# First feed-forward product by seven block products: weight-block sums on VectorE, residual rows on GpSimd

## The chip, the cores and the metric

One core of a Trainium2 chip runs the whole kernel. The metric is device time in microseconds (us) of one execution; the profile beside it is one execution taken by the hardware profiler.

## The reference

One decoder layer over 512 tokens of width 2048, all in float32. The change touches the second half, from the first normalisation to the hidden layer of the feed-forward part:

```python
        x = layer_norm(DEEPNORM_ALPHA * x + mix, ln_mix_g[layer], ln_mix_b[layer])
        f = jnp.square(jax.nn.relu(x @ w_ff1[layer])) @ w_ff2[layer]
        x = layer_norm(DEEPNORM_ALPHA * x + f, ln_ff_g[layer], ln_ff_b[layer])
```

Here x is 512 x 2048, `w_ff1` 2048 x 8192 and `w_ff2` 8192 x 2048. Ahead of it stand the input product, two token mixers (attention and pooling), the gates and the output product.

## The kernel before

**Split products.** Every float32 operand of a large product is split into a high part (an fp32r copy made on ScalarE, line 86) and a low part (operand minus high part, on VectorE, line 87). A product is three matmuls: high x high, high x low, low x high. Weights stream through `wr` (loaded on SP's queue), `wh` and `wl`, three buffers of each. A step of a product takes two 128-row slices of weight by 512 columns, 24 matmuls. `fill` issues the split of step i + 2 ahead of the matmuls of step i, so the third buffer comes free when the matmuls of step i - 1 end. `late` is a list of closures; one is popped in each step. The order on each engine is the order in which the code is written.

**First feed-forward product (line 146).** 16 groups of 512 hidden channels. A group is 16 slices of the contraction x 4 blocks of 128 channels x 3 = 192 matmuls, weights stationary, the 512 tokens moving. Group 0 is done in two halves of 256 tokens (`F[0]`, `F[1]`), while the first normalisation (`ln1_norm`, transposes `ln1_t`) of the other half runs beside it. When a group ends, `ff1_evac` takes four PSUM tiles through Relu and Square on ScalarE into `hpR`, and puts two closures on `late`. Each (`parts`) makes four sums of 256 columns on VectorE (line 498), a high part `hpH` of 7 x 256 columns on ScalarE, a low part `hpL` on VectorE, and two stores to `h_parts` on GpSimd's DMA queue. The last two groups need no sums (`plain_parts`).

**Second product (line 615).** It reads `h_parts` back and already works by 2 x 2 x 2 blocks with seven products for seven chunks of 1024 hidden channels; the last chunk (line 660) is plain. Its weight sums are VectorE operations on 128 x 2048 (lines 585 to 596).

**Residual.** `ln1_finish` multiplies and adds the normalisation's weights to `acc` in natural layout on VectorE (line 479), and `y_save` stores the rows to `y_parts` with some columns subtracted; they seed the accumulators of the second product.

Everything is one program order per engine; nothing is reordered.

Of the kernel before, what the change touches and what calls it, by code (L numbers as in the profile page):

```python
# [35 lines left out]
C_MADD, C_CNT, C_ID, C_RC, C_IF, C_W = 0, 512, 1024, 1152, 1216, 1217  # L36

# [30 lines left out]
def decoder_layer(ctx: ExitStack, tc: tile.TileContext, x, xt, positions, w_in, w_pool, pool_scale,  # L68
                  w_branch_attn, w_branch_pool, w_out, ln_mix_g, ln_mix_b, w_ff1, w_ff2,
                  ln_ff_g, ln_ff_b, consts, vectors, out, h_parts, h_rest, y_parts):  # L70
# [6 lines left out]
    cst = G.tile([P, C_W], F32, name="cst")  # L77
# [5 lines left out]
    ident = cst[:, C_ID:C_ID + P]  # L83
# [9 lines left out]
    # ---------------------------------------------------------------- streamed products  # L93
# [101 lines left out]
    # ---------------------------------------------------------------- x, given transposed  # L195
    L1s = ExitStack()
    L1 = L1s.enter_context(tc.tile_pool(name="L1", bufs=1))
    xs = []
# [15 lines left out]
    # ---------------------------------------------------------------- queue of all products  # L214
# [6 lines left out]
    # pooling branch  # L221
# [33 lines left out]
    def pool_diff(g):  # L255
        s, u = pooled[g], uu.pop(g)
        d = s
        rc = cst[:, C_RC + 16 * g:C_RC + 16 * g + 16]
# [32 lines left out]
    # attention  # L291
    rope = {}

    def rope_tables():
# [4 lines left out]
        nc.vector.tensor_scalar(ang, ang, cst[:, C_IF:C_IF + 1], None, op0=OP.mult)  # L299
# [45 lines left out]
    def s1a(i):  # L345
# [7 lines left out]
        nc.vector.tensor_add(sm[i][:, :n], p[:, :n], cst[:, o:o + n])  # L353
# [4 lines left out]
    def s1b(i):  # L358
# [3 lines left out]
        nc.vector.scalar_tensor_tensor(sm[i][:, :n], sm[i][:, :n], 1.0, cst[:, o:o + n], op0=OP.mult,  # L362
# [71 lines left out]
    # output projection, residual and normalisation  # L434
# [19 lines left out]
    def ln1_norm(t0):  # L454
        for t in (t0, t0 + 1):
            ln_stat(t)
        for t in (t0, t0 + 1):
            nc.vector.tensor_scalar(acc[t], acc[t], mv[:, t, 0:1], mv[:, t, 3:4],
                                    op0=OP.subtract, op1=OP.mult)

    def ln1_t(t0, j):
        p = PS.tile([P, 2, 2 * P], F32, name="sc" if j % 2 else "tp", bufs=1)
        y = L2["p"].tile([P, 2, 2 * P], F32, name="rl", bufs=2)
        for e in range(2):
            k = 2 * j + e
            for t in range(2):
                nc.tensor.transpose(p[:, e, t * P:(t + 1) * P], acc[t0 + t][:, k * P:(k + 1) * P], ident)  # L467
        for e in range(2):
# [9 lines left out]
    def ln1_finish(t, op, v):  # L478
        nc.vector.tensor_tensor(acc[t], acc[t], L2[v], op=op)

    def y_save(t):
        if t < 2:
            for n in (1, 3):
                c = slice(n * 512, (n + 1) * 512)
                nc.vector.tensor_tensor(acc[t + 2][:, c], acc[t + 2][:, c], acc[t][:, c], op=OP.subtract)
        nc.gpsimd.dma_start(y_parts[t], acc[t])
# [4 lines left out]
    # the hidden layer: its blocks (tokens x channels) 11 12 21 22 and the sums that the second product takes  # L491
    # slots: 21, 11, 22, 12, then S1 = 21 + 22, S2 = S1 - 11, S3 = 11 - 21, S4 = 12 - S2; the last chunk needs no sums
    def ff1_evac(g):
        def parts(j):
            a, b, c = ("h1", "h2", "h3") if j else ("h4", "h5", "h6")
            r = R[j]
            for d, x0, x1, op in ((4, 0, 2, OP.add), (5, 4, 1, OP.subtract), (6, 1, 0, OP.subtract), (7, 3, 5, OP.subtract)):
                nc.vector.tensor_tensor(r[:, d], r[:, x0], r[:, x1], op=op)
            h = L2["p"].tile([P, 7, 256], F32R, name="hpH", tag=b)
            l = L2["p"].tile([P, 7, 256], F32R, name="hpL", tag=c)  # L500
            split(h, l, r[:, 1:])
            for e, v in enumerate((h, l)):
                nc.gpsimd.dma_start(h_parts[g // 2, e, :, :, 2 * (g % 2) + j].rearrange("s p f -> p s f"), v.bitcast(F32))

        def plain_parts():
            h = L2["p"].tile([P, 2, 4, 256], F32R, name="hpH", tag="h5")
            l = L2["p"].tile([P, 2, 4, 256], F32R, name="hpL", tag="h6")
            split(h, l, R["all"])
            for e, v in enumerate((h, l)):
                for j in range(2):  # L510
                    nc.gpsimd.dma_start(h_rest[e, :, :, 2 * (g % 2) + j], v[:, j].bitcast(F32))

        R = {}

        def f(b, p):
            if not R:
                if g < 14:
                    for j in range(2):
                        R[j] = L2["p"].tile([P, 8, 256], F32, name="hpR", tag=("h4", "h1")[j])
                else:  # L520
                    R["all"] = L2["p"].tile([P, 2, 4, 256], F32, name="hpR", tag="h4")
                    R[0], R[1] = R["all"][:, 0], R["all"][:, 1]
            t = lambda b: R[b % 2][:, 2 * (b // 2):2 * (b // 2) + 2]
            nc.scalar.activation(t(b), p, AF.Relu)  # L524
            if b == 3:
                for b in range(4):
                    nc.scalar.activation(t(b), t(b), AF.Square)
                late.extend([lambda: parts(0), lambda: parts(1)] if g < 14 else [plain_parts])
# [3 lines left out]
    # second product, by blocks of 2 x 2 x 2 with seven products  # L532
    MO = (("11", 1), ("21", 3), ("22", 7), ("11", 4), ("E", 6), ("22", 5), ("21", 2))
    first_tags = {"11": "w0", "21": "w1", "22": "w2", "12": "w3", "E": "w4"}
# [3 lines left out]
    def h_load(c, m):  # L538
        v = L2["p"].tile([P, 2, 4, 256], F32R, name="hop", tag=f"h{m}")
# [4 lines left out]
    def w_rows(c, k):  # L544
        """Rows of the second weight that block row k of chunk c takes: two tiles from each group of 512."""
        return w_ff2[c * 1024:(c + 1) * 1024].rearrange("(a k b p) n -> k p a b n", a=2, k=2, b=2)[k]

    class Unit:
# [11 lines left out]
        def give(self, role, new):  # L560
            """The tile of a role that is done goes to a role of the next unit."""
# [67 lines left out]
    def bcast(v):  # L629
        return bass.AP(tensor=v.tensor, offset=v.offset, ap=[[0, P], [1, DM]])  # L630

    def tail_load(m):
        if m < 4:
            rest[m] = L2["p"].tile([P, 2, 4, 256], F32R, name="hop", tag=f"h{m}")
            for e in range(2):
                nc.gpsimd.dma_start(rest[m][:, e], h_rest[e, :, m])
        elif m < 6:
            rest[m] = L2["p"].tile([P, DM], F32, name="ln", tag=f"h{m}")
# [38 lines left out]
    def block(t, n):  # L677
        """Row t, columns n * 512 on of the sum that the last normalisation takes."""
# [18 lines left out]
    # ---------------------------------------------------------------- the order of the products  # L697
# [20 lines left out]
    F += [add(cols(w_ff1, n * 512), 16, "ws", yact, ff1_evac(n)) for n in range(1, 16)]  # L718
# [5 lines left out]
    units[0].tag = dict(first_tags)  # L724
# [5 lines left out]
    steps += pieces + ends  # L730

    # ---------------------------------------------------------------- emission
# [172 lines left out]
```

## Time and profile before

| | |
|---|---|
| median of 3 runs | 2449.92 us (2448.81 to 2450.59) |
| span of the profiled execution, first to last instruction | 2448.5 us |
| PE busy | 2433.2 us, 99% |
| VectorE (DVE) busy | 1303.0 us, 53% |
| ScalarE (ACT) busy | 851.9 us, 35% |
| GpSimd (POOL) busy | 130.7 us, 5% |
| matmuls | 10936 |
| moved by DMA | 383.29 MB, mean 157 GB/s |

For the profiled execution the span is the time that is given; it lies 1.4 us (0.06%) under the median. PE is TensorE's matmuls, PEld its weight loads, SP and POOL also issue DMAs. PE counts as busy from a matmul's start to its modelled end, and matmuls overlap, so what one costs is read from the distance of two starts.

### The profile page before, as it was taken

How to read it: one execution, taken by the hardware profiler on the slowest of the kernel's cores; microseconds unless marked ns; L12 is line 12 of the kernel's file. 1: busy time of each engine (PE TensorE's matmuls, PEld its weight loads, DVE VectorE, ACT ScalarE, POOL GpSimd, SP SyncE). 2: the span in 40 equal slices, each digit the busy share in tenths (PEclk: the TensorE clock that was granted, in tenths of full speed). 3: DMA queues.
4: the chain of work that ended last, by engine and by line, in shares of the span. 5: the costliest groups of instructions: out<-in, count | busy, mean ns of one | idle time of the engine just before them, and what ended most of it. 6: DMA issues, size and time to landing. Idle time of an engine off the chain costs nothing.

```text
span 2448.5 us, 26732 instructions
## 1 busy us (share of the span) xinstructions
PE 2433.2 (99%) x10936; PEld 2010.9 (82%) x10936; DVE 1303.0 (53%) x1409; ACT 851.9 (35%) x952; POOL 130.7 (5%) x188
## 2 busy tenths in 40 slices
PE   9999999999999999999999999999999999999998
PEld 7888888877788888889888888888888888888886
DVE  4532245555522335356653334343347988889887
ACT  4323321244422222137434333343334333333330
POOL 0000000000000000000110101000021000110000
PEclk9999999999999999999999999999999999999999
DMA  6333333322233333465665645546677457575652
GB/s 217 87 94 99 103 96 95 95 78 78 71 93 97 101 95 116 125 198 167 195 243 166 217 155 196 183 160 210 241 262 261 160 186 240 206 240 168 210 164 94
DMA packets 166842, 383.29 MB, mean 157 GB/s; under 512 B 11200, under 2 KB 12224, under 8 KB 165696
## 3 DMA queue, kind: packets, MB, share of 16 engines
q1 hardware_dynamic: 133408, 257.84, 33.5%
q0 software_dynamic: 30720, 117.45, 13.8%
q10 hardware_dynamic: 2592, 6.29, 0.8%
q8 instruction: 86, 1.41, 0.2%
q14 instruction: 36, 0.29, 0.0%
HBM read 317.58 MB, written 63.96 MB: 156 GB/s over the span
## 4 chain that ended last, share of the span: by engine, by line
PE 97%; DVE 1%; DMA 1%; ACT 0%; issue 0%; SPq 0%; POOLq 0%; DVEq 0%
PE mm L146 71%; PE pp L615 20%; PE pp L660 4%; PE sc L349 1%; PE tp L381 1%; DMA w<-in_w_ff 1%; DVE wl L87 0%; PE tp L373 0%; PE tp L275 0%; PE sc L275 0%; DVE part L621 0%; DMA wr<-in_w_in 0%; PE sc L467 0%; PE tp L467 0%; ACT wh L86 0%
## 5 line engine op out<-in xcount | busy, mean ns | idle before, releaser
L87 DVE TENSOR_TENSOR wl<-wr,wh 128x1024 fp32r<-128x1024 f32 (+1 forms) x348 | 423.3, 1221 | 891.5 <-ACT wh L86 890.9
L146 PE MATMUL mm<-aH,wh 128*128 128x512 f32 (+1 forms) x1984 | 768.8, 387 | 0.8 <-ACT wh L86 0.6
L146 PE MATMUL mm<-aH,wl 128*128 128x512 f32 (+1 forms) x1984 | 759.4, 383 | 0.2 <-DVE wl L87 0.2
L146 PE MATMUL mm<-aL,wh 128*128 128x512 f32 (+1 forms) x1984 | 758.7, 382 | 0.0
L86 ACT ACTIVATE wh<-wr 128x1024 fp32r<-128x1024 f32 (+1 forms) x348 | 367.0, 1055 | 878.2 <-PE mm L146 809.0
L615 PE MATMUL pp<-wh,hop 128*128 128x512 f32 x1568 | 483.1, 389 | 0.7 <-ACT hpR L524 0.7
L146 PEld LDWEIGHTS mm<-aH,wh 128*128 128x128 f32 x1984 | 373.2, 188 | 76.4 <-ACT wh L86 2.3
L146 PEld LDWEIGHTS mm<-aL,wh 128*128 128x128 f32 x1984 | 373.2, 188 | 74.3 <-issue 1.9
L146 PEld LDWEIGHTS mm<-aH,wl 128*128 128x128 f32 x1984 | 373.0, 188 | 73.9 <-DVE wl L87 1.1
L615 PEld LDWEIGHTS pp<-wh,hop 128*128 128x128 f32 x1568 | 294.4, 188 | 62.0 <-ACT hpR L524 1.1
L86 ACT ACTIVATE wh<-w 128x1024 fp32r<-128x1024 f32 x196 | 208.1, 1062 | 313.6 <-PE pp L615 295.5
L615 PE MATMUL pp<-wl,hop 128*128 128x512 f32 x784 | 305.2, 389 | 1.0 <-DVE wl L87 1.0
L87 DVE TENSOR_TENSOR wl<-w,wh 128x1024 fp32r<-128x1024 f32 x196 | 238.4, 1222 | 71.4 <-ACT wh L86 64.3
L615 PEld LDWEIGHTS pp<-wl,hop 128*128 128x128 f32 x784 | 147.2, 188 | 32.4 <-DVE wl L87 1.9
L146 PE MATMUL mm<-wh,aH 128*128 128x512 f32 x384 | 149.9, 390 | 0.0
L146 PE MATMUL mm<-wl,aH 128*128 128x512 f32 x384 | 149.5, 389 | 0.0
L146 PE MATMUL mm<-wh,aL 128*128 128x512 f32 x384 | 149.5, 389 | 0.0
L621 DVE TENSOR_TENSOR part<-part,pp 128x1024 f32<-128x1024 f32 x92 | 112.1, 1218 | 12.7 <-PE pp L615 12.7
L87 DVE TENSOR_TENSOR hpL<-hpR,hpH 128x1792 fp32r<-128x1792 f32 (+1 forms) x30 | 61.3, 2044 | 52.1 <-ACT hpH L86 52.1
L146 PEld LDWEIGHTS mm<-wl,aH 128*128 128x128 f32 x384 | 72.1, 188 | 15.2 <-DVE wl L87 0.4
L146 PEld LDWEIGHTS mm<-wh,aL 128*128 128x128 f32 x384 | 72.1, 188 | 15.1
L146 PEld LDWEIGHTS mm<-wh,aH 128*128 128x128 f32 x384 | 72.1, 188 | 14.7
(143 smaller groups left out, 1700.1 us busy)
## 6 DMA issues: line engine op xcount, KB each, us to landing
wr<-in_w_ff SPq DMA_DIRECT2D x152, 512.0 KB, 3.9
wr<-in_w_in SPq DMA_DIRECT2D x127, 512.0 KB, 3.7
w<-in_w_ff SPq DMA_DIRECT2D x112, 512.0 KB, 6.1
hop<-h_parts POOLq DMA_DIRECT2D x98, 512.0 KB, 7.2
h_parts<-hpH POOLq DMA_DIRECT2D x28, 896.0 KB, 5.7
h_parts<-hpL POOLq DMA_DIRECT2D x28, 896.0 KB, 7.7
wr<-in_w_out SPq DMA_DIRECT2D x40, 512.0 KB, 3.7
wr<-in_w_branch_pool SPq DMA_DIRECT2D x16, 512.0 KB, 3.6
```

Source lines behind the costliest of these rows:

```text
L86: nc.scalar.activation(dst_h, src, AF.Copy)
L87: nc.vector.tensor_tensor(dst_l, src, dst_h.bitcast(F32), op=OP.subtract)
L146: nc.tensor.matmul(o, l, r, start=first and j == 0, stop=last and j == 2)
L349: nc.tensor.matmul(p[:, :n], qT[h][:, qb * P:(qb + 1) * P], kT[h][:, :n], start=True, stop=True)
L381: nc.tensor.matmul(p[:, k * P:], vt["v"][:, k, h * HD:(h + 1) * HD], pT[h][:, k, k * P:], start=k == 0, stop=k == 3)
L615: nc.tensor.matmul(u.ps[:, t], l, r, start=q + j == 0, stop=q == 3 and j == 2)
L621: nc.vector.tensor_tensor(p, p, u.ps, op=OP.add)
L660: nc.tensor.matmul(o, l, r, start=first and i == 0, stop=last and i == 2)
```

## The change

Groups 1 to 15 of the first feed-forward product are computed by 2 x 2 x 2 blocks: the tokens in halves of 256, the contraction in halves of 1024, the group's channels in halves of 256. Seven products M1 to M7 take the place of eight. Each is 2 pieces of 24 matmuls with 256 moving columns.

- The activation sums P1 to P4 are made once, in `F[1]` (`y_sums`, `y_p3`), on VectorE and ScalarE.
- The weight sums are made in each group, four additions of 128 x 2048 on VectorE in place (`sum`). Weight blocks are loaded as 1024 x 256 tiles (`get`, `give`); the tile of a block that is done goes to the next group.
- Products accumulate in three PSUM banks: M1, M6, M7 and M4 in one, M5 and M3 in the second, M2 in the third. In between, a bank's sum so far is copied out (`evac`: M1, M5 and M6 by a ScalarE copy, M7 by a VectorE operation).
- Group 1 takes the products in the order `ORDER1`, groups 2 to 15 in `ORDER`.
- The split of the hidden layer's parts (`h_parts_out`) keeps its operations; `hpH` now has one buffer (tag t10) for all, and the low part is written over `hpR`.
- `ln1_finish` and `y_save` go. The normalised rows are stored to `y_norm`, and `y_rows` loads 128 x 512 chunks of them back and finishes them on GpSimd, 16 chunks in groups 1 to 9.
- The attention masks get a tile of their own, and tags of the tiles are renamed.

```diff
+        k, c0 = int(role[0]) - 1, self.g * 512 + (int(role[1]) - 1) * 256
+        nc.sync.dma_start(self.b[role], w_ff1[k * 1024:(k + 1) * 1024, c0:c0 + 256].rearrange("(a p) n -> p a n", p=P))
...
-    def ln1_finish(t, op, v):
-        nc.vector.tensor_tensor(acc[t], acc[t], L2[v], op=op)
...
+    def y_sums():
+
+        return [lambda: (y_add("22", "22", "21", OP.subtract), y_sum("P1", "22")),
+                lambda: (y_add("21", "11", "21", OP.subtract), y_add("11", "11", "22", OP.add)),
+                lambda: (y_add("12", "11", "12", OP.subtract), y_sum("P2", "11")),
+                lambda: y_sum("P4", "12")]
...
+    def y_rows(t, n):
+        c = slice(n * 512, (n + 1) * 512)
+        v, g, b = low["u"][:, 1], low["g"][:, 0], low["g"][:, 1]
+        tt = nc.gpsimd.tensor_tensor
+        nc.gpsimd.dma_start(v, y_norm[t, :, c])
...
+        tt(v, v, g, op=OP.mult)
+        tt(v, v, b, op=OP.add)
+        nc.gpsimd.tensor_scalar(v, v, ALPHA, None, op0=OP.mult)
+        if t >= 2 and n % 2:
+            nc.gpsimd.dma_start(g, y_parts[t - 2, :, c])
+            tt(v, v, g, op=OP.subtract)
+        nc.gpsimd.dma_start(y_parts[t, :, c], v)
...
+    def h_parts_out(g, j):
+        r = R[g][:, j]
+        for d, x0, x1, op in ((4, 0, 2, OP.add), (5, 4, 1, OP.subtract), (6, 1, 0, OP.subtract), (7, 3, 5, OP.subtract)):
+            nc.vector.tensor_tensor(r[:, d], r[:, x0], r[:, x1], op=op)
+        h = L2["p"].tile([P, 7, 256], F32R, name="hpH", tag="t10")
+        split(h, r[:, 1:], r[:, 1:])
+        for e, v in enumerate((h.bitcast(F32), r[:, 1:])):
+            nc.gpsimd.dma_start(h_parts[g // 2, e, :, :, 2 * (g % 2) + j].rearrange("s p f -> p s f"), v)
...
+    ORDER = ("M1", "M2", "M5", "M3", "M6", "M7", "M4")
+    ORDER1 = ("M1", "M5", "M6", "M3", "M7", "M2", "M4")
+    FACTORS = {"M1": ("11", "11"), "M5": ("P1", "11"), "M6": ("P2", "11"), "M3": ("P4", "22"), "M7": ("P3", "12"),
+               "M2": ("12", "21"), "M4": ("22", "11")}
...
+            split(self.h, self.l, b[FACTORS[self.what][1]][:, 4 * (j % 2):4 * (j % 2) + 4])
+            if j % 2:
+                for o, i in {"M1": (("11", "12"),), "M5": (("11", "22"),), "M6": (("11", "21"),)}.get(self.what, ()):
+                    u.sum(o, i)
+            elif self.what == "M3":
+                u.sum("12", "22")
...
+            p = u.ps[{"M3": "M5", "M2": "M2", "M5": "M5"}.get(what, "M1")]
+            for n in range(2):
+                o = p[:, n * 256:(n + 1) * 256]
+                for k in range(4):
...
+            def block(slot, in0, in1, op):
+                r = R[u.g][:, :, slot]
+                tt(r, in0.rearrange("p (n t) -> p n t", n=2), in1, op=op)
+                act(r, r, AF.Relu)
+
+            if what == "M1":
+                act(m1, ps["M1"], AF.Copy)
+            elif what == "M5":
+                act(m5, ps["M5"], AF.Copy, scale=-1.0)
+            elif what == "M6":
+                act(u2, ps["M1"], AF.Copy, scale=-1.0)
+            elif what == "M3":
+                h_rows(u.g)
+            elif what == "M7":
+                block(3, m5, v["M1"], OP.subtract)
+            elif what == "M4":
+                act(R[u.g][:, :, 1], v["M1"], AF.Relu)
+                act(R[u.g][:, :, :4], R[u.g][:, :, :4], AF.Square)
+                late.extend(h_out(u.g))
...
+    for p in fpieces:
+        fill(pos[2])
+        if late:
+            late.pop(0)()
+        if p.u is funits[0] and p.j == 0:
+            y_p3()
+            funits[0].get("21")
+        p.mult()
+        pos[2] += 1
+        if p.j == 2 and chunks:
+            y_rows(*chunks.pop(0))
+        elif p.j == 8 and chunks and p.u.g < 8:
+            y_rows(*chunks.pop(0))
```

Three places in the engines' orders. First VectorE's order around the end of a group in the middle of the first product, before: `wl` is the low part of the weights, `hpR` takes the four sums, `hpL` is the low part of the hidden layer's parts.

```order
L87 TENSOR_TENSOR wl<-wr,wh 128x1024 x7
L498 TENSOR_TENSOR hpR<-hpR 128x256 x4
L87 TENSOR_TENSOR hpL<-hpR,hpH 128x1792
L87 TENSOR_TENSOR wl<-wr,wh 128x1024
L498 TENSOR_TENSOR hpR<-hpR 128x256 x4
L87 TENSOR_TENSOR hpL<-hpR,hpH 128x1792
L87 TENSOR_TENSOR wl<-wr,wh 128x1024 x7
```

The same place now, from the end of group 6 on; `w_10296` and the like are the weight blocks, `low` holds the copies of banks, L608 is the sum of two weight blocks.

```order
L90 TENSOR_TENSOR wl<-w_10296,wh 128x1024 x2
L608 TENSOR_TENSOR w_10296<-w_10296,w_10424 128x2048
L90 TENSOR_TENSOR wl<-w_10356,wh 128x1024
L543 TENSOR_TENSOR hpR<-hpR 128x256 x4
L90 TENSOR_TENSOR hpR<-hpR,hpH 128x1792
L90 TENSOR_TENSOR wl<-w_10356,wh 128x1024
L543 TENSOR_TENSOR hpR<-hpR 128x256 x4
L90 TENSOR_TENSOR hpR<-hpR,hpH 128x1792
L90 TENSOR_TENSOR wl<-w_10296,wh 128x1024 x2
L608 TENSOR_TENSOR w_10296<-w_10296,w_10485 128x2048
L90 TENSOR_TENSOR wl<-w_10485,wh 128x1024
L608 TENSOR_TENSOR w_10424<-w_10424,w_10485 128x2048
```

The pieces' low parts, the two bundles of parts and their order are as before; the weight sums stand between them, and each `wl` now feeds 24 matmuls of 256 columns in place of 24 of 512.

Second, TensorE's order in group 6 now: the last matmul of M5 and the first of M3, then the same of M6 and M7, of M7 and M4, with what a row waits for; the numbers name buffers, `mm_10267` and `mm_10134` are banks, `ysH` and `aH` high parts of activations.

```order
L646 MATMUL mm_10267<-ysH_7700,wl_10234 128x256
L646 MATMUL mm_10267<-ysH_7799,wh_10262 128x256 [waits Activation_49]
...
L646 MATMUL mm_10134<-ysH_7767,wl_10352 128x256
L646 MATMUL mm_10134<-aH_5948,wh_10385 128x256 [waits Activation_49]
...
L646 MATMUL mm_10134<-aH_5988,wl_10421 128x256
L646 MATMUL mm_10134<-aH_6028,wh_10453 128x256 [waits DVE_49,Activation_49]
```

Each pair adds to the same bank, and between the two the bank is read: by ScalarE's copies of `mm_10267` and of `mm_10134` in the first two pairs, by VectorE's operation on `mm_10134` in the third. Before, a bank was read only when its group had ended, and the next group took other banks.

Third, GpSimd's queue behind the stores of a group's parts, now; before, only stores and loads stood there.

```order
L547 DMA h_parts<-hpR 128x7x256
L522 DMA low<-y_norm 128x512
L523 DMA low<-in_ln_mix_g 128x512
L524 DMA low<-in_ln_mix_b 128x512
L525 TENSOR_TENSOR low<-low 128x512
L526 TENSOR_TENSOR low<-low 128x512
L527 TENSOR_SCALAR low<-low 128x512
L531 DMA y_parts<-low 128x512
```

Two such chunks follow each other in groups 1 to 7, one in groups 8 and 9; four of the sixteen also load an earlier chunk and subtract it.

## Rows read from the trace of the kernel before

**Rows 1.** The page: busy time, the granted clock in 40 slices, the chain.

```profile
PE 2433.2 (99%) x10936; PEld 2010.9 (82%) x10936; DVE 1303.0 (53%) x1409; ACT 851.9 (35%) x952; POOL 130.7 (5%) x188
...
PEclk9999999999999999999999999999999999999999
...
PE 97%; DVE 1%; DMA 1%; ACT 0%; issue 0%; SPq 0%; POOLq 0%; DVEq 0%
```

**Rows 2.** Timeline of PE in the first product: start us, us, instruction.

```profile
1145.86 0.28 PE L146 MATMUL mm<-aH,wh 128*128 128x256 f32 x1
...
1161.21 0.28 PE L146 MATMUL mm<-aH,wl 128*128 128x256 f32 x1
1161.34 0.40 PE L146 MATMUL mm<-aH,wh 128*128 128x512 f32 x1
...
1813.93 0.39 PE L146 MATMUL mm<-aH,wl 128*128 128x512 f32 x1
```

**Rows 3.** Timeline where the first product ends and the second begins, all engines.

```profile
1814.36 0.60 ACT L524 ACTIVATE hpR<-mm 128x512 f32<-128x512 f32 x1 [0.27 <-PE mm L146]
...
1815.01 0.50 PE L615 MATMUL pp<-wh,hop 128*128 128x512 f32 x1 [0.69 <-ACT hpR L524]
...
1817.89 1.91 ACT L86 ACTIVATE hpH<-hpR 128x2048 fp32r<-128x2048 f32 x1
```

**Rows 4.** Timeline of PE, ACT and DVE around the end of group 4.

```profile
1335.44 0.39 PE L146 MATMUL mm<-aH,wh 128*128 128x512 f32 x1
...
1335.64 0.60 ACT L524 ACTIVATE hpR<-mm 128x512 f32<-128x512 f32 x1 [0.27 <-PE mm L146]
1336.14 2.18 ACT L527 ACTIVATE hpR<-hpR 128x512 f32<-128x512 f32 x4
1338.22 1.05 ACT L86 ACTIVATE wh<-wr 128x1024 fp32r<-128x1024 f32 x1
...
1348.52 1.70 ACT L86 ACTIVATE hpH<-hpR 128x1792 fp32r<-128x1792 f32 x1 [3.79 <-issue]
...
1339.30 1.23 DVE L87 TENSOR_TENSOR wl<-wr,wh 128x1024 fp32r<-128x1024 f32 x1 [7.00 <-ACT wh L86]
1340.44 1.55 DVE L498 TENSOR_TENSOR hpR<-hpR 128x256 f32<-128x256 f32 x4
1343.81 2.03 DVE L87 TENSOR_TENSOR hpL<-hpR,hpH 128x1792 fp32r<-128x1792 f32 x1 [1.82 <-ACT hpH L86]
1345.75 1.22 DVE L87 TENSOR_TENSOR wl<-wr,wh 128x1024 fp32r<-128x1024 f32 x1
...
1350.25 2.03 DVE L87 TENSOR_TENSOR hpL<-hpR,hpH 128x1792 fp32r<-128x1792 f32 x1 [1.82 <-ACT hpH L86]
1352.19 2.35 DVE L87 TENSOR_TENSOR wl<-wr,wh 128x1024 fp32r<-128x1024 f32 x2
```

**Rows 5.** Timeline of POOL there, and from the page the stores' time to landing.

```profile
1344.07 0.99 POOL L503 DMA_DIRECT2D h_parts<-hpH  x1 [34.03 <-ACT hpH L86]
...
h_parts<-hpH POOLq DMA_DIRECT2D x28, 896.0 KB, 5.7
```

**Rows 6.** Groups of instructions by line and shape: count, busy us, mean ns, idle before.

```profile
L596 DVE TENSOR_TENSOR w<-w,w 128x2048 f32<-128x2048 f32 x14 | 32.0, 2289 | 0.0
...
L683 DVE TENSOR_TENSOR part<-part,pp 128x512 f32<-128x512 f32 x8 | 5.5, 685 | 10.2 <-PE pp L660 10.2
```

**Rows 7.** The same view: GpSimd's one kind of arithmetic, in both normalisations.

```profile
L450 POOL TENSOR_TENSOR mv<-mv,nh 128x1 f32<-128x1 f32 x8 | 9.8, 1228 | 1202.4 <-DVE mv L449 1202.4
```

**Rows 8.** Stretches: length, then busy us (instructions) of PE, PEld, DVE, ACT, POOL; clock.

```profile
1400.00:1800.00 400.00, 400.00 (x1766) 331.20 (x1766) 145.94 (x155) 143.79 (x163) 38.95 (x44) 1.00 0.61 202
...
2000.00:2300.00 300.00, 300.00 (x1325) 248.51 (x1324) 261.50 (x197) 117.23 (x111) 29.54 (x56) 1.00 0.61 206
```

**Rows 9.** PE's last matmul; a later stretch: length, PE busy, granted clock, DMA.

```profile
2436.73 0.39 PE L660 MATMUL pp<-wh,hop 128*128 128x512 f32 x1
...
2440.00:2440.50 0.50, 0.00 (x0) 0.76 0.00 0
```

More of the change, by code (lines that the diff above doesn't have):

```diff
@@ L476, in ln1_side, with y_add @@
         return [lambda: ln1_norm(t0)] + [lambda j=j: ln1_t(t0, j) for j in range(8)]
-    def ln1_finish(t, op, v):
-        nc.vector.tensor_tensor(acc[t], acc[t], L2[v], op=op)
[L481 to L486, printed above, removed]
+    def y_add(out, a, b, op):
+        nc.vector.tensor_tensor(yr[out], yr[a], yr[b], op=op)
@@ L488, in yact @@
     def yact(k):
         return yH[k // 4][:, k % 4, :], yL[k // 4][:, k % 4, :]
-    def ff1_evac(g):
[L494 to L513, printed above, removed]
-        def f(b, p):
[L516 to L524, printed above, removed]
@@ new lines, in h_plain_out, with h_out, h_rows @@
+    def h_plain_out(g):
+        h = L2["p"].tile([P, 2, 4, 256], F32R, name="hpH", tag="t10")
+        r = R[g][:, :, :4]
+        split(h, r, r)
+        for j in range(2):
+            for e, v in enumerate((h[:, j].bitcast(F32), r[:, j])):
+                nc.gpsimd.dma_start(h_rest[e, :, :, 2 * (g % 2) + j], v)
+    def h_out(g):
+        return [lambda: h_parts_out(g, 0), lambda: h_parts_out(g, 1)] if g < 14 else [lambda: h_plain_out(g)]
+    def h_rows(g):
+        R[g] = L2["p"].tile([P, 2, 8, 256], F32, name="hpR", tag="R")
@@ L525, in f @@
+    def ff1_evac(g):
+        def f(b, p):
+            if g not in R:
+                h_rows(g)
+            t = R[g][:, b % 2, 2 * (b // 2):2 * (b // 2) + 2]
+            nc.scalar.activation(t, p, AF.Relu)
+            nc.scalar.activation(t, t, AF.Square)
             if b == 3:
-                for b in range(4):
-                    nc.scalar.activation(t(b), t(b), AF.Square)
-                late.extend([lambda: parts(0), lambda: parts(1)] if g < 14 else [plain_parts])
-        return f
+                late.extend(h_out(g))
+        return f
@@ new lines, in decoder_layer, with __init__, get, sum @@
+    class FUnit:
+        def __init__(self, g):
+            self.g, self.b, self.tag, self.next, self.ps = g, {}, {}, None, {}
+            self.products = ORDER1 if g == 1 else ORDER
+            self.freed = ("22", "12", "21", "11") if g == 1 else ("22", "21", "12", "11")
+        def get(self, role):
+            self.b[role] = L2["p"].tile([P, 8, 256], F32, name="w1", tag=self.tag[role])
+            k, c0 = int(role[0]) - 1, self.g * 512 + (int(role[1]) - 1) * 256
+            nc.sync.dma_start(self.b[role], w_ff1[k * 1024:(k + 1) * 1024, c0:c0 + 256].rearrange("(a p) n -> p a n", p=P))
+        def sum(self, role, other):
+            W_ADD(self.b[role], self.b[role], self.b[other], op=OP.add)
+        def give(self, role, new):
+            self.next.tag[new] = self.tag[role]
+            self.next.get(new)
@@ L723, in decoder_layer @@
         a.next = b
-    units[0].tag = dict(first_tags)
+    for a, b in zip(funits, funits[1:] + units[:1]):
+        a.next = b
+        a.order = ("11", "21", "22", "12") if b is units[0] else ("11", "12", "21", "22") if a is funits[0] else ("11", "21", "12", "22")
+    funits[0].tag = {"11": "t0", "12": "t2", "22": "t3", "21": "t1"}
+    units[0].tag = {"E": "t10"}
+    fpieces = [FPiece(u, j) for u in funits for j in range(14)]
     pieces = [Piece(u, j) for u in units for j in range(14)]
@@ L729, in decoder_layer @@
     ends = [Last(j) for j in range(16)]
-    steps += pieces + ends
+    steps += fpieces + pieces + ends
     TA, TB, TC = [None], [None], [None]
```

126 lines of the change are left out of this document (94 added, 32 removed).

## Prediction

> **What bounds the kernel now.** I read the page first: PE is busy 99% of the span, the chain of what ended last is 97% PE, and the granted clock is at its upper level, 2.4 GHz, in all 40 slices [rows 1]. So the question is what PE's columns cost in the first product, and then whether PE would still be the last to be ready there. In the timeline of PE the 2880 matmuls of groups 1 to 15 start between 1161.34 and 1813.93 us: (1813.93 - 1161.34) / 2879 = 0.2267 us each [rows 2]. A group of 192 takes 43.5 us, the fifteen 652.8 us. The engines beside it have room: from 1400 to 1800 us VectorE is busy 146 of 400 us and ScalarE 144, while PE has no gap [rows 8]. That is an average over a group; what matters here is one place in it, the end of a group, and there I read the timeline of all three engines [rows 4].
>
> **PE's columns.** The trace before holds the new shape already: the 256-column matmuls of group 0. 129 of them start from 1145.86 to 1161.21 us, 15.35 / 128 = 0.1199 us each [rows 2]. A group becomes 7 products x 2 pieces x 24 = 336 of these, 40.3 us. Saved: 43.5 - 40.3 = 3.2 us a group, 48.4 us in fifteen. A piece, the unit in which weights are split, shrinks from 5.44 us to 24 x 0.1199 = 2.88 us, while its split on ScalarE and VectorE costs what it did (1.05 and 1.2 us).
>
> **Three banks that are read between products.** In groups 2 to 15 M3 follows M5 at once in the same bank, M7 follows M6, M4 follows M7, and each time the bank must be read out in between. The price of such a turn stands at the end of the first product [rows 2, 3]: the last matmul starts at 1813.93, ScalarE's Relu from PSUM runs from 1814.36 for 0.60, PE goes on at 1815.01. A 256-column matmul lasts 0.28 in place of 0.39, so from the last start to the next it is 0.28 + 0.04 + 0.60 + 0.05 = 0.97, less the 0.12 that it takes anyway: 0.85 us. The turn over VectorE takes 0.685 for the operation on a bank [rows 6], 0.94 us. Together 2 x 0.85 + 0.94 = 2.64 us a group, in 14 groups 37.0 us. Group 1 has another product between the two in each case. The lower bound is nothing, if the copies were hidden, but PE's order has nothing between the two products that it could do instead, and the waits stand in it.
>
> **The end of a group.** This is the largest term. ScalarE and VectorE go through one chain there, and the change keeps its order: Relu and Square, the high and low part of piece 2, four sums, `hpH`, the low part, piece 3, the same bundle again, piece 4. The trace before shows when each link ends [rows 4]. The next group's first matmul starts at 1335.44. The low part of piece 2 ends at 1339.30 + 1.23, 5.1 us after it; that of piece 3 at 1345.75 + 1.22, 11.5 us after; that of piece 4, the first of two from 1352.19 on, 18.0 us after. Before, PE comes to these pieces after 10.9, 16.3 and 21.8 us and waits for none. With pieces of 2.88 us it comes to them after 5.8, 8.6 and 11.5 us. One thing is added: `hpH` has a single buffer now, so the second one, which started at 1348.52, waits until the first has been stored. That store was issued at 1344.07 and lands in 5.7 us [rows 5], at 1349.8, so 1.25 us later: piece 4 is ready 19.2 us after the group's start.
>
> The low part is first needed by a piece's third matmul, 0.24 us in. Piece 3: 11.5 - (8.63 + 0.24) = 2.65 us late. From there PE needs 22 matmuls and 0.24 us, 2.88 us, to the same point of piece 4: 19.2 - 14.4 = 4.85 us late. Together 7.5 us in each group that starts with two bundles, groups 2 to 14: 13 x 7.5 = 97.5 us. Later in the group VectorE catches up, by my count from the same durations: four weight sums of 2.29 us [rows 6] and eight splits fit between piece 5 and the end, with 1.2 us to spare at piece 7 and 2 to 3 us after it. The sum of weight blocks for the next group ends before ScalarE has the high part of piece 2, so it adds nothing to the chain.
>
> **From group 0 to group 1.** Seven operations of 128 x 2048 for the activation sums (2.29 each), the bundles of group 0, the split for P3 and the first weight sums crowd here. From the start of step 3 of `F[1]` I go down VectorE's order: 2.5 us to the first low part; an addition, ScalarE's copy of 1.91 [rows 3] and a low part, 9.0; a split, 10.2; two additions, 14.8; a split, 16.0; an addition and a low part, 20.6; then split, P4's low part, split, weight sum, split, 28.8; a bundle (5.4, hand-overs included), 34.2; P3's split, 36.7; split and weight sum, 40.2; a bundle, 45.6; the split of group 1's piece 4, 46.8. PE comes to that after nine pieces, 9 x 2.88 + 0.24 = 26.1. It is 20.7 us late. `ln1_finish` and `y_save`, which go, took VectorE's time under full PE and give back nothing.
>
> **The clock.** PE stands still for 4 to 5 us at piece 4 of each group. The one place where the trace shows the clock fall is the end: the last matmul starts at 2436.73 and ends 0.39 later, and the stretch from 2440.0 to 2440.5 is granted 0.76, a fall from 1 to 0.5 at 2440.26, so 3.1 us after PE stopped [rows 9]. The new gaps are longer than that but broken by two matmuls, so I charge the fall in half of the groups, at one piece that runs at 1.2 in place of 2.4 GHz: 7 x 2.88 = 20.2 us. The bounds are 0 and 14 x 2.88 = 40 us. The Trainium skill (TensorE: Matmul & The Clock Gate, Why this matters for your kernels) advises against idle gaps between bursts of matmuls, as they throw the clock back; by it the fall comes in every group, and the sum would be 20 us higher.
>
> **GpSimd.** 16 chunks, 52 operations on 128 x 512. The trace has no such row; the nearest is 1.23 us for 128 x 1 [rows 7], so three operations take at least 3.7 us. They start after the stores of a group's second bundle, where VectorE is 1.2 to 3 us ahead of PE. If VectorE stood still for their whole length, 3.7 - 1.2 = 2.5 us would show in each of groups 2 to 9, 20 us. The lower bound is 0, as no row shows VectorE held up by GpSimd; I take 0 and keep the 20 as a rival. The Trainium skill (SBUF — State Buffer, Who interferes with whom) says that a VectorE instruction with two SBUF inputs and a GpSimd instruction that reads SBUF shut each other out for the whole instruction. By that rule the 20 us are due, since nearly all of VectorE's operations here have two SBUF inputs.
>
> **Sum.** -48.4 + 37.0 + 97.5 + 20.7 + 20.2 = +127.0 us. The profiled span is 2448.5, 1.4 us below the median, and the change is set on the median: 2449.9 + 127.0 = 2577 us. Weight loads are no term: as many bytes as before, and each block is asked for at least four pieces (11 us) ahead.
>
> **Rivals.**
> *The chain does not reach PE (faster).* For it speaks that from 2000 to 2300 us VectorE is busy 261 of 300 us, with the same kind of weight sums, and PE has no gap [rows 8]. Then only the banks cost: 2449.9 - 48.4 + 37.0 = 2438.5 us. It decides at about 11.4 us of waiting in all, under 0.9 us a group: the links to piece 4 would have to take 11.5 us and not 19. Against it stands that the same links in the same order took 18.0 us before. Chance 0.08.
> *Neither chain nor banks are seen.* 2449.9 - 48.4 = 2401.5 us. Chance 0.02.
> *The gain and the waits cancel.* The wait is about 1 us a group. Chance 0.02.
> *More is late.* The clock falls in every group (+20), GpSimd holds VectorE up in eight groups (+20), and stores land 1 to 2 us later because more is loaded beside them, which moves piece 4 by as much (+13 to +26): up to 2577 + 66 = 2643 us, about 2620 with two of them. Chance 0.18.
>
> **How the numbers follow.** My forecast, with the chain on the path, has 0.70; its own range is 2557 (the clock never falls) less 20 for links that run a little shorter, to 2610. The range with 8 in 10 takes the upper rival in to 2630 and leaves the faster ones out: 2530 to 2630 us. Less than 0.2%, 5 us, is about what a measurement of this kernel can't tell from no change. Faster 0.09, same 0.03, slower 0.88.
>
> **What would show it.** Right: matmuls of 256 columns 0.12 us apart inside a piece; a group of about 50 us; PE idle twice at the start of a group, released by VectorE's low part (and ScalarE's high part), 7 to 8 us together; three gaps of 0.9 us released by the copies of banks; about 20 us around the first group; the clock below 1 in the first product. Group 1 should show no bank gaps, and group 15, which follows a group without sums, no long wait. Wrong: a group of 43 us or less, a bundle of parts that takes under 3 us, or PE waiting for GpSimd or a DMA.

## The result, and the profile after

The changed kernel takes 2578.07 us (median of 4 runs, 2577.53 to 2581.51) against 2450.26 for the kernel before beside it: a ratio of 1.0521, 95% interval 1.0506 to 1.0536. The forecast was 2577. The profiled execution has a span of 2579.6 us, 131.1 more than the one before; the spans of the other three runs are 2575.5, 2576.0 and 2576.0, 3.6 to 4.1 us less; where most of that may lie is said below.

The page of the changed kernel, with the rows that answer to [rows 1]:

```profile
PE 2454.9 (95%) x13096; PEld 2122.1 (82%) x13096; DVE 1581.8 (61%) x1601; ACT 964.3 (37%) x1045; POOL 258.8 (10%) x308
...
PEclk9999999999999999998989999999899999999999
```

PE is still busy 95%, but a busy share counts a slow matmul as well as a fast one, and the clock row now has eights within the first product. What PE waited for there (us in total, times, longest us) stands in the view of waits; line 646 is the matmul of the block products:

```profile
PE mm L646 <- DVE wl L90: 45.0, 30, 2.4
PE mm L646 <- ACT wh L89: 25.2, 28, 3.1
PE mm L646 <- DVE hpR L659: 12.7, 14, 1.3
PE mm L646 <- ACT low L667: 9.6, 14, 0.7
PE mm L646 <- ACT low L665: 9.6, 14, 0.7
```

The first two are the chain at the start of a group (low and high part of the weights), the last three the banks, 14 times each. Group 12 shows where; PE's timeline, its first matmul, all that it waited for, and the first matmul of group 13:

```profile
1746.94 0.28 PE L646 MATMUL mm<-aH,wh 128*128 128x256 f32 x1
...
1756.14 0.39 PE L646 MATMUL mm<-aH,wh 128*128 128x256 f32 x1 [0.40 <-ACT wh L89]
...
1758.39 0.58 PE L646 MATMUL mm<-aH,wl 128*128 128x256 f32 x1 [1.75 <-DVE wl L90]
...
1763.48 0.39 PE L646 MATMUL mm<-ysH,wh 128*128 128x256 f32 x1 [0.88 <-ACT wh L89]
...
1765.24 0.58 PE L646 MATMUL mm<-ysH,wl 128*128 128x256 f32 x1 [1.26 <-DVE wl L90]
...
1773.01 0.39 PE L646 MATMUL mm<-ysH,wh 128*128 128x256 f32 x1 [0.69 <-ACT low L665]
...
1785.47 0.38 PE L646 MATMUL mm<-aH,wh 128*128 128x256 f32 x1 [0.69 <-ACT low L667]
...
1792.36 0.36 PE L646 MATMUL mm<-aH,wh 128*128 128x256 f32 x1 [0.87 <-DVE hpR L659]
...
1798.18 0.28 PE L646 MATMUL mm<-aH,wh 128*128 128x256 f32 x1
```

The group takes 51.24 us. Its 336 matmuls at 0.12 make 40.32, the banks 2.96 (0.93, 0.93 and 1.10: from the turns' start-to-start distances over 0.12, and the piece behind each), and 7.94 us are lost at pieces 2 to 4. The idle times printed add up to less than that, because the matmuls between them run at the lower clock. The links answer to [rows 4]; ScalarE and VectorE in the same group:

```profile
1757.11 1.22 DVE L90 TENSOR_TENSOR wl<-w,wh 128x1024 fp32r<-128x1024 f32 x1
...
1760.30 1.70 ACT L89 ACTIVATE hpH<-hpR 128x1792 fp32r<-128x1792 f32 x1 [4.21 <-DMA h_parts<-hpH]
...
1763.97 2.36 DVE L90 TENSOR_TENSOR wl<-w,wh 128x1024 fp32r<-128x1024 f32 x2
```

Piece 3's low part ends 11.4 us after the group's start (forecast 11.5), piece 4's, the first of two, about 18.2 (forecast 19.2). ScalarE waits for the store of the first `hpH`, the single buffer's price. Groups 2 to 14 take 51.2 to 52.6 us, and in each of them the granted clock is at its lower level, 1.2 GHz, for 6.8 us. Group 15, which follows a group without sums, takes 43.5, and group 1 59.9.

### The profile page after: what moved, and what is told of

Its sections match the earlier page's. It is cut to its first block, busy times and chain, and to the rows that moved or that the text cites. A ratio compares the mean times of both kernels' runs of the same rounds, so it can differ in the third digit from the quotient of the medians.

```text
span 2579.6 us, 31523 instructions
## 1 busy us (share of the span) xinstructions
PE 2454.9 (95%) x13096; PEld 2122.1 (82%) x13096; DVE 1581.8 (61%) x1601; ACT 964.3 (37%) x1045; POOL 258.8 (10%) x308
## 5 line engine op out<-in xcount | busy, mean ns | idle before, releaser
L90 DVE TENSOR_TENSOR wl<-w,wh 128x1024 fp32r<-128x1024 f32 x406 | 498.9, 1238 | 229.2 <-ACT wh L89 229.2
L89 ACT ACTIVATE wh<-w 128x1024 fp32r<-128x1024 f32 x406 | 424.3, 1055 | 432.8 <-PE pp L764 294.4
L149 PE MATMUL mm<-aH,wh 128*128 128x512 f32 (+1 forms) x1024 | 396.5, 387 | 1.5 <-ACT wh L89 1.5
L149 PE MATMUL mm<-aH,wl 128*128 128x512 f32 (+1 forms) x1024 | 387.0, 378 | 5.1 <-DVE wl L90 5.1
L149 PE MATMUL mm<-aL,wh 128*128 128x512 f32 (+1 forms) x1024 | 386.3, 377 | 0.0
L646 PE MATMUL mm<-aH,wh 128*128 128x256 f32 x960 | 283.5, 295 | 29.5 <-DVE hpR L659 12.7
L646 PE MATMUL mm<-aH,wl 128*128 128x256 f32 x960 | 282.4, 294 | 25.1 <-DVE wl L90 25.1
L646 PE MATMUL mm<-aL,wh 128*128 128x256 f32 x960 | 279.4, 291 | 0.0
L646 PE MATMUL mm<-ysH,wh 128*128 128x256 f32 x720 | 216.8, 301 | 27.6 <-ACT wh L89 18.0
L646 PE MATMUL mm<-ysH,wl 128*128 128x256 f32 x720 | 216.1, 300 | 19.9 <-DVE wl L90 19.9
```

The source lines that it names most:

```text
L89: nc.scalar.activation(dst_h, src, AF.Copy)
L90: nc.vector.tensor_tensor(dst_l, src, dst_h.bitcast(F32), op=OP.subtract)
L149: nc.tensor.matmul(o, l, r, start=first and j == 0, stop=last and j == 2)
L646: nc.tensor.matmul(o, l, r, start=first, stop=self.j % 2 == 1 and k == 3 and i == 2, skip_group_check=True)
```

## Experiments

Main theory: PE is held up at the start of each group by one chain through VectorE and ScalarE (bundle of the hidden layer's parts, then the split of the weights), then by three bank turns. Rivals: VectorE has too much to do wherever the work stands; GpSimd or the clock is the cause.

**1. No bundles.** In place of the four sums, `hpH` and the low part, in groups 0 to 13:

```diff
...
+        for e in range(2):
+            for s, v in ((0, r[:, :4]), (4, r[:, 1:4])):
+                nc.gpsimd.dma_start(h_parts[g // 2, e, s:s + v.shape[1], ...], v)
```

> Leaves out the four sums, the high and the low part of the hidden layer's parts in groups 0 to 13 (the stores write the blocks themselves, so h_parts holds other numbers). If the chain of these links is what PE waits for: a group of 43.3 us (40.3 of columns, 3.0 of bank turns) in place of 51.3, 13 x 8.0 = 104 us less, and some 10 us less in group 1, whose VectorE loses two bundles: about 2464 us, with the clock at 1 throughout. Rival, VectorE is too full for pieces of 2.88 us whatever the bundle does (weight sums and splits alone): groups stay above 47 us, over 2515 us.

Measured: 2474.76 us, ratio 1.0101 (1.0072 to 1.0131). Two groups' first matmuls:

```profile
1662.46 0.28 PE L643 MATMUL mm<-aH,wh 128*128 128x256 f32 x1
...
1705.76 0.28 PE L643 MATMUL mm<-aH,wh 128*128 128x256 f32 x1
```

A group is 43.30 us, columns and banks and nothing else, and its clock stays at 1. The chain with what it does to the clock is therefore the whole 7.9 us. The run is 11 us slower than I expected, for two waits of its own. Group 8 took 47.6 us, with one wait of 3.7 us for a bank's copy. Group 1 takes 55.4 us, 4.4 less and not 10. Up to the end of its piece 4, where all its loss had been, it does lose far less, 6.8 us in place of 19.5 (`F[1]` takes 1.4 us longer in this trace). But 8.3 us are lost anew at piece 6, where VectorE waits for the load of a weight block:

```profile
1196.52 2.29 DVE L605 TENSOR_TENSOR w<-w,w 128x2048 f32<-128x2048 f32 x1 [7.55 <-DMA w<-in_w_ff]
```

The load went out at 1182.06, just behind eight stores of parts, and took 14.4 us to land, against 7.8 for the same block in the changed kernel; that the stores are the reason was not tested. So the bundles are the larger part of the crowd in group 1, as expected.

**2. The same bundles, spread.** The two of a group are cut into five closures, one a piece, and the residual chunks move from pieces 2 and 8 to pieces 5 and 11:

```diff
...
-        return [lambda: h_parts_out(g, 0), lambda: h_parts_out(g, 1)]
+        return [lambda: h_sums(g, 0), lambda: (h_high(g, 0), h_sums(g, 1)), lambda: h_low(g, 0),
+                lambda: h_high(g, 1), lambda: h_low(g, 1)]
...
-        if p.j == 2 and chunks:
+        if p.j == 5 and chunks:
             y_rows(*chunks.pop(0))
-        elif p.j == 8 and chunks and p.u.g < 8:
+        elif p.j == 11 and chunks and p.u.g < 8:
```

> Same work, but each bundle in five closures, one a piece: sums; high part and the second sums; low part; second high part; second low part. The residual chunks move from pieces 2 and 8 to 5 and 11, so that the stores do not queue behind them. If it is the place of the bundles ahead of the splits that makes PE wait, and not their length: VectorE has 35.5 us of work in a group of 43.3, the wait falls from 8.0 to about 2 us a group and the clock stays up: 13 x 6 = 78 us less, about 2500 us. Rival, VectorE simply has too much to do in the first seven pieces (22.6 us of work for 20.2 us of matmuls), so that the wait moves to pieces 5 to 7: less than 30 us gained, above 2548 us.

Measured: 2523.65 us, ratio 1.0301 (1.0271 to 1.0331), between the two. Groups 9 to 13 take 44.8 to 45.3 us, so there the chain is gone with all its work still done, and it was the place. Groups 2 to 8 take 47 to 54 us, for a reason neither theory had: the residual chunks, which this edit moved, now run beside the next group's bundles. Group 5 on ScalarE, VectorE and GpSimd:

```profile
1377.53 3.63 DVE L543 TENSOR_TENSOR hpR<-hpR 128x256 f32<-128x256 f32 x4
...
1377.64 1.46 POOL L525 TENSOR_TENSOR low<-low 128x512 f32<-128x512 f32 x1 [3.67 <-DMA low<-in_ln_mix_g]
1379.44 1.42 POOL L526 TENSOR_TENSOR low<-low 128x512 f32<-128x512 f32 x1 [0.34 <-DMA low<-in_ln_mix_b]
...
1389.01 0.56 POOL L531 DMA_DIRECT2D y_parts<-low  x1 [0.30 <-POOL low L530]
1389.56 0.95 POOL L548 DMA_DIRECT2D h_parts<-hpH  x1
...
1394.61 1.70 ACT L552 ACTIVATE hpH<-hpR 128x1792 fp32r<-128x1792 f32 x1 [9.29 <-DMA h_parts<-hpH]
```

The store of `hpH` stands behind a residual chunk on GpSimd's in-order queue and goes out at 1389.56, though `hpH` was done at 1382.9. ScalarE waits 9.29 us for its landing, with the splits of the weights behind it. In groups 2, 4, 5 and 8 this store goes out 2.7 to 6.6 us after `hpH` is done. In groups 3, 6 and 7 it goes out at once, but GpSimd's operations lie beside the first four sums on VectorE, which take 2.0 to 4.0 us there and 1.55 in groups 9 to 14, where no chunk meets them. How much each of the two costs was not tried apart. Group 14, which has no chunk, took 47.5 us and was not taken apart.

**3. No bank turns.** Group 1's order of the products for all groups (`self.products = ORDER1`).

> Group 1's order of the products in all groups, bundles as they are. The three bank gaps go: 14 x 2.96 = 41 us less. But in this order the second weight sum (2.29 us) stands behind the split of piece 3, ahead of the second bundle and the split of piece 4. Theory (one chain on VectorE): piece 4 is 2.29 us later in 13 groups, 30 us back, so about 2567 us, with the wait at piece 4 grown by about 2.3 us and no bank gaps. Rival (the sum is hidden in a wait for ScalarE or the store): all 41 us are gained, 2537 us.

Measured: 2579.22 us, ratio 1.0528 (1.0497 to 1.0558): nothing gained. The bank gaps are gone, and the view of waits holds little beside the chain:

```profile
PE mm L646 <- ACT wh L89: 53.5, 30, 4.1
PE mm L646 <- DVE wl L90: 44.9, 32, 2.8
```

Here is why; VectorE and ScalarE in group 12 (starts at 1747.66):

```profile
1759.08 2.29 DVE L608 TENSOR_TENSOR w<-w,w 128x2048 f32<-128x2048 f32 x1
1761.29 1.55 DVE L543 TENSOR_TENSOR hpR<-hpR 128x256 f32<-128x256 f32 x4
...
1762.92 1.70 ACT L89 ACTIVATE hpH<-hpR 128x1792 fp32r<-128x1792 f32 x1 [6.12 <-DVE hpR L543]
```

A weight sum of 2.29 us has come into the chain ahead of the second bundle. The loss at pieces 2 to 5 rises from 7.9 to 10.9 us, just what the banks gave. The rival (all 41 us gained) falls. My own number was off by 12 us: the loss grew by 2.9 us a group and not 2.29, and groups 4 and 8 took 2.6 and 1.2 us longer than in the changed kernel. The clock is at its lower level for 10.2 us of group 12 in place of 6.8, which may hold the other 0.6; that was not taken apart.

**4 and 5. Does the clock matter?** Matmuls with unused results fill part of the waits:

```diff
...
+                        if u.g > 1 and self.j in (3, 4) and n + k == 0 and i == 2:
+                            q = PS.tile([P, 512], F32, name="sc", bufs=1)
+                            for _ in range(28 if self.j == 3 else 20):
+                                nc.tensor.matmul(q[:, :256], ...)
```

> In groups 2 to 15, 28 matmuls of 256 columns into an idle bank ahead of the third matmul of piece 3 and 20 ahead of that of piece 4 (3.4 and 2.4 us, within the waits of 4.5 and 2.9 us), their results unused. If standing still is what lowers the clock: no stretch at 0.5 at pieces 3 and 4, 1.4 us less in a group, 19 us in all, about 2559 us. Rival, the clock falls for another reason or costs nothing because the pieces wait anyway: no change, 2575 to 2581 us; or the filler holds up PE: longer.

Measured: 2574.18 us, ratio 1.0507 (1.0477 to 1.0538). The clock no longer falls in groups 2 to 15, but a group becomes only 0.4 us shorter, which could pass for the clock's price. It is not: the loss at piece 4 was 2.49 us, the length of the filler's 20 matmuls. In group 15, which has no such wait, the filler added 5.6 us. Hence the second run, with 10 matmuls at piece 4 and `1 < u.g < 15`.

> As the first run with unused matmuls, but 10 instead of 20 ahead of piece 4's third matmul (1.2 us) and none in group 15. In the first run the wait at piece 4 was 2.49 us, which is just the length of its 20 matmuls, so that run could not show a shorter one. If the lowered clock costs what the trace of the changed kernel suggests (1.4 us a group): the waits are 0.56 + 4.48 + about 1.5, a group of 49.8 us, about 2558 us. Rival, the data come at 2.49 us whatever PE does: a group of 50.8 us, about 2571 us.

Measured: 2565.67 us, ratio 1.0470 (1.0454 to 1.0485). The same stretches of group 12 in the view of stretches (length; PE busy and matmuls; granted clock; DMA share; GB/s), first of the changed kernel, then of this one:

```profile
1758.00:1761.00 3.00, 2.61 (x12) 0.50 0.94 320
1762.00:1764.00 2.00, 1.10 (x8) 1.00 0.32 115
1765.00:1768.00 3.00, 2.76 (x13) 0.50 0.93 318
```

```profile
1749.00:1752.00 3.00, 3.00 (x27) 1.00 0.93 318
1756.00:1759.00 3.00, 2.93 (x25) 1.00 0.95 320
```

At 1.2 GHz PE starts 12 or 13 matmuls in 3 us in place of 25 to 27. A group is 49.93 us, 1.3 less, with losses of 0.56, 4.46 and 1.63 at pieces 2 to 4. So standing still is what lowers the clock, in every group, and it costs 1.3 us a group net: the first of the two slow pieces costs nothing, since PE waits at its end anyway. Groups 4 to 8 of this run took 50.7 to 52.7 us (in group 6 the first `hpH`'s store landed later, ScalarE waited 5.88 us for it), so the total is 8 us above what I expected.

**6. GpSimd without arithmetic.** The four operations of `y_rows` go.

> Leaves out GpSimd's arithmetic on the residual chunks (y_parts then holds the plain normalised rows); its loads and stores stay. If GpSimd hardly holds up VectorE at the place that counts, as groups 2 to 9 against 10 to 14 say: 3.5 us less, about 2574 us. Rival, VectorE and GpSimd shut each other out for whole operations (52 of 1.4 to 1.9 us): 20 us less, about 2558 us.

Measured: 2579.65 us, ratio 1.0526 (1.0510 to 1.0542): no gain that can be measured. In the traces groups 2 to 9 take 410.0 us instead of 413.4, the 3.4 us expected, but groups 10 to 14, which have no chunk in either kernel, take 3.1 more, so a difference of this size is not clear of what groups vary by. The rival of 20 us falls.

**7 and 8. Group 1 in the old form.** One more plain group ahead of the block groups:

```diff
...
+         add(cols(w_ff1, 512), 16, "ws", yact, ff1_evac(1))]
+    funits = [FUnit(g) for g in range(2, 16)]
```

> Group 1 is computed as before the change, 192 matmuls of 512 columns, with group 0's bundles and P3 beside it; blocks begin with group 2. If the 19.5 us of waiting in group 1 are the crowd on VectorE, a group of 43.5 us has room for it: 59.9 becomes 43.5, 16.4 us less, about 2562 us. Rival, the crowd moves with it: waits of 5 us or more in group 1, about 2568 us or more.

Measured: 2574.43 us, ratio 1.0505 (1.0484 to 1.0526). P3 was made in the middle of group 1, over activations that the rest of the group read (so the rest used other numbers), and PE waited 5.9 us for it: the edit brought a wait of its own and tells nothing of the crowd. With P3 behind group 1:

> Group 1 as before the change (192 matmuls), and P3 made after it, since P3 is written over activations that group 1 still reads; in the earlier run with a plain group 1 P3 came in its middle and PE waited 5.9 us for it. Group 2 takes the products in the order that group 1 had. If the 19.5 us of waiting in group 1 are the crowd on VectorE, they go, for 3.2 us of columns, and group 2 has the 8 us of any group with two bundles: about 2562 us. Rival, the waits come back in group 2, with P3 at its start: 2570 us or more.

Measured: 2566.59 us, ratio 1.0477 (1.0456 to 1.0498). Group 2 now starts at 1214.24 instead of 1231.06, 16.8 us earlier, but `F[1]` already starts 3.1 us earlier (1139.42 instead of 1142.56), which lies ahead of all that this edit touches. From there to group 2 it is 13.7 us less where 16.4 were expected, so most of the waits of group 1 are the crowd. Groups 2 to 14 give 5.3 us back: 1.4 in group 2, where P3 now is, the rest in groups of 52 to 53 us. So the time lies between theory and rival.

**9 to 12. A version without the chain.** Each step of these four was chosen from the trace of the one before. All compute group 1 in the old form, take `ORDER1`, and spread the bundles; the first has P3 where run 7 had it, with the same effect on its numbers.

> Group 1 plain; group 1's old order of products for all block groups, so no bank is read between two neighbours; bundles in five closures, each behind a split; the second and third block's read-outs and the last two weight sums where VectorE has time (after products 5 and 4); the high part's store on ScalarE's queue instead of GpSimd's; one residual chunk a group at piece 5, two in groups 2 and 3. Theory: VectorE's order and GpSimd's queue were the cause, so a group falls to 40.3 to 41.5 us: 2578 - 772 + 43.5 + 14 x 40.4 to 41.5 = 2415 to 2430 us. Rival, VectorE with 35.5 us of work in 40.3 us and GpSimd beside it has no such order: over 3 us of waiting left in a group, above 2455 us.

Measured: 2531.12 us, ratio 1.0340 (1.0320 to 1.0360); groups of 46 to 50 us. ScalarE in group 12:

```profile
1769.15 1.70 ACT L552 ACTIVATE hpH<-hpR 128x1792 fp32r<-128x1792 f32 x1 [4.88 <-DVE hpR L543]
...
1779.40 2.01 ACT L89 ACTIVATE wh<-w 128x1024 fp32r<-128x1024 f32 x2 [5.13 <-DVE w L620]
```

Both wait for an instruction of VectorE that was issued just ahead of them, and the weights' high parts queue behind the first or are themselves the second. The rival is right for this order, not for any: the next ones move each `hpH` to a later step than its sums.

> As the combined version, with P3 after group 1, and so ordered that no operation of ScalarE stands right behind one of VectorE that it needs: sums, high part and low part of a bundle in three different pieces, the second bundle from piece 4 on, the third weight sum at piece 5, all three read-outs into the hidden layer's tile after product 6, the residual chunk at piece 8, the activation sums spread over the end of group 0 and group 1. Theory (in the combined version ScalarE waited 4.9 us for the second bundle's sums and 5.1 us for a weight sum, with the splits behind it): a group falls from 47.8 to about 41.6 us, some 6 us less in group 0: about 2430 us, below the kernel before. Rival, VectorE's 22.6 us of work up to piece 8 are too much in any order: 2 to 3 us of waiting stay in a group, 2440 to 2465 us.

Measured: 2485.39 us, ratio 1.0147 (1.0130 to 1.0164); nine of 14 groups 43.0 to 44.3 us, with 0.2 to 1.1 us lost at nearly every piece from 4 on. That is 2.7 to 4.0 us a group, so the rival holds for these groups. The total lies 20 us above its range: two waits of 7 us, in the first block group and at the start of the second product, were for stores, and four more groups took 45 to 47 us.

> As the second combined version, with the bundles later and further apart (first sums at piece 1, high part at 3, low part and second sums at 5, second high and low part at 7), the fourth weight sum at piece 8, group 0's bundles earlier within group 1, no residual chunk in the last group (three groups have two). Theory (what is left in the second version, 3 us in a group of 43.3, is order: ScalarE waits 4.0 us for the second sums, weight sums and bundles stand close together; the 7 us ahead of the first block group are group 1's tile waiting for a store, the 7 us at the start of the second product a store behind a residual chunk on GpSimd's queue): a group of 40.3 to 41.3 us, 28 to 42 us less in 14 groups, and 10 to 15 us less around them: 2485 - 38 to 57 = 2428 to 2447 us. Rival, VectorE's 35.5 us of work in 40.3 us, held up by GpSimd, is the bound: groups stay at 43 us or more, about 2470 us.

```diff
...
+        return [nop, f[0], nop, f[1], nop, lambda: (f[2](), f[3]()), nop, lambda: (f[4](), f[5]())]
```

(`f` holds sums, high and low part of the first bundle, then of the second.) Measured: 2447.99 us against 2450.8, ratio 0.999 (0.9981 to 0.9999): no more than level with the kernel before. Twelve of 14 groups take 41.5 to 43.8 us, most of them between what the theory and what the rival asked for. What is left is mostly one wait, PE's for VectorE's read-out of a bank ahead of the last product; group 3, which has the longest of them and a lower clock behind it, took 51.0 us.

```profile
PE mm L662 <- DVE hpR L675: 20.6, 14, 6.5
PE mm L662 <- DVE wl L90: 7.5, 9, 1.6
```

> As the third combined version, with two things changed. The stores of the low parts go from GpSimd's queue to ScalarE's, one piece after the low part is made, so that the hidden layer's tile does not wait for residual chunks. Two of the three read-outs into that tile come after the first half of product 2 instead of its end, so that the last product's bank is free in time. Theory (in the third version PE waits 20.6 us in 14 groups for VectorE's read-out ahead of the last product, up to 6.5 us, and for little else): these go, a group falls from 42.6 to about 41 us, about 2430 us, 0.8% under the kernel before. Rival, VectorE, now fuller, passes the wait on to the splits: 2440 to 2448 us.

Measured: 2507.82 us, ratio 1.0238 (1.0224 to 1.0252): 60 us slower than the third version. The wait grew, because the tile that the read-out writes into (`hpR`) comes free only when its store has landed:

```profile
PE mm L662 <- DVE hpR L675: 51.2, 13, 9.3
...
1732.00 1.29 DVE L675 TENSOR_TENSOR hpR<-low,mm 128x512 f32<-128x512 f32 x2 [5.98 <-DMA h_parts<-hpR]
```

The pages' stores (count, KB each, median us to landing), of the third version and then of the fourth:

```profile
h_parts<-hpR POOLq DMA_DIRECT2D x28, 896.0 KB, 8.9
```

```profile
h_parts<-hpR ACTq DMA_DIRECT2D x28, 896.0 KB, 10.5
```

The same store, now on ScalarE's queue, takes longer to land, it goes out a piece later, and VectorE needs the tile 2.9 us earlier; the three were not tried apart. Both the theory and its rival missed.

## Why the prediction was right, point by point

In the end the terms, as the prediction named them, against what was measured (us):

| term | predicted | measured | from |
|---|---|---|---|
| columns | -48.4 | -48.0 | 336 x 0.1200 a group |
| three bank turns | +37.0 | +41.4 | 14 x 2.96; gone in run 3 |
| chain at a group's end | +97.5 | +86.5 | 13 x 6.65, run 5 |
| clock | +20.2 | +16.8 | 13 x 1.29, run 5 against the changed kernel |
| GpSimd | 0 | +3.4 | groups 2 to 9 in run 6, not clear of noise |
| group 0 to group 1 | +20.7 | +23.8 | `F[1]` 4.3 longer, group 1 19.5 over its columns |
| ahead of `F[1]` | none | +2.5 | not foreseen |
| start of the kernel | none | +3.1 | not foreseen |
| second product and after | none | +1.2 | 635.5 against 634.3 |
| sum | +127.0 | +130.7 | spans: +131.1 |

The forecast is 1 us from the time, and that is luck: the terms missed by 15 us upwards, without the start, and by 14 downwards. The mechanism was right in kind: every term that was forecast is there with its sign, and nothing else that is large.

**The chain** was read rightly from [rows 4]: the same links, in the same order, 11.4 and 18.2 us after a group's start. It came 0.8 us a group smaller because the first `hpH`'s store landed in 4.8 us, not the 5.7 of [rows 5], and ScalarE waited less. Run 1 shows that it is the whole loss, run 2 that it is a matter of place.

**The banks** cost 0.32 us a group more than 2.64. The turns themselves were 0.84, 0.84 and 1.03; the step had left out that the piece behind each turn takes 0.07 to 0.09 longer.

**The clock** was mis-sized in both of its factors, which nearly cancelled: it falls in each of groups 2 to 14, not in half of them, but costs 1.3 us and not 2.88, since one of its two slow pieces lies ahead of a wait. The picture of one still-stand of 4 to 5 us was wrong too: the waits are spread over pieces 3 and 4, and in group 12 the clock falls although no single one is longer than 1.75 us. The Trainium skill (TensorE: Matmul & The Clock Gate, Why this matters for your kernels) advises against idle gaps between bursts of matmuls. The fall in every group that I read from it came; the 40 us did not, and the trace decides: 16.8.

**GpSimd** was taken at nothing because no row showed it holding VectorE up. It does hold VectorE up (last section), but here mostly where VectorE has time; run 2 shows what it costs where VectorE has none.

**The transition** fits, its inner sum too. Run 1 takes the two bundles out, and `F[1]` and group 1 up to the end of piece 4 lose 11.4 us less, where the prediction's walk has two of 5.4; the load that then came late is not in the walk. Of what was not foreseen, 1.4 of the 2.5 us ahead of `F[1]` come where ScalarE waits 5.1 us for a load of the output product's weights (0.6 before), while two of the new stores of normalised rows run, and 1.1 in `F[0]`, behind VectorE's normalisation; neither was tested. The 3.1 us at the start belong to the profiled execution and not to the change: its first step ran 10 matmuls in the stretch from 8 to 12 us in place of 18, and runs 1, 2 and 4, which have the same start, ran 18 there. The spans of the other three executions are 3.6 to 4.1 us shorter, which fits, though they have no trace.

## What to carry to other kernels

A cheaper matmul shortens the time that everything beside it has: before counting its columns, follow each engine's program order through the tightest stretch with the new piece length, because a mean load (VectorE 61% here) says nothing of it. Then ask of every instruction that waits what is queued behind it: here ScalarE's `hpH` held up the weights' high parts three times: it waited for a buffer, for a store behind GpSimd's arithmetic, and for VectorE's sums of the same step. Removing a wait that PE shows (the banks, 41 us) gained nothing as long as the cure lengthened the chain ahead of it.

## What the runs showed of the hardware

VectorE and GpSimd hold each other up. In run 2 four additions that take 1.55 us took 3.63 beside two GpSimd operations (the rows there). In group 8 of the changed kernel a low part of 1.22 us took 1.99:

```profile
1544.18 1.29 POOL L530 TENSOR_TENSOR low<-low 128x512 f32<-128x512 f32 x1 [3.07 <-DMA low<-y_parts]
...
1544.56 1.99 DVE L90 TENSOR_TENSOR wl<-w,wh 128x1024 fp32r<-128x1024 f32 x1 [1.48 <-ACT wh L89]
```

It ends 1.08 us after GpSimd's operation does. The other way round, of the 16 additions of line 526 on GpSimd the eleven that began while a low part of line 90 was under way on VectorE took 2.13 to 2.31 us, the other five 1.29 to 1.30. The Trainium skill (SBUF — State Buffer, Who interferes with whom) says that the ports which the two share are an exclusive lock, and that a VectorE instruction with two SBUF inputs contends with a GpSimd instruction that reads SBUF; these rows agree. What it costs depends on where they meet: no gain could be measured without GpSimd's arithmetic (run 6), while in run 2 it more than doubled sums on the chain.

GpSimd's additions and multiplications on 128 x 512 take 1.3 us undisturbed and the scaling 1.5, hardly more than the 1.23 us for 128 x 1 of [rows 7]. And a store's time to landing is no constant: `hpH`'s 896 KB took 5.7 us before, 4.8 after (medians of 28), and 4.1, 6.4, 7.4 and 6.6 on ScalarE's queue in the four versions of runs 9 to 12. So that queue alone does not make it longer; what does was not tested.
